# Two transformer blocks: small projections from unpadded weights, an earlier forget gate, and edits at the start, the norms, the second attention and the end

## The chip, the cores and the metric

The kernel runs on one core of a Trainium2 chip. Its time is the device time of one launch in microseconds; the median of three runs was 2513.2 (2512.42 to 2513.47).

## The reference

Two blocks in sequence on x of 256 tokens by 2048 channels, in fp32.

```python
# first block
h = rmsnorm(x, g_mix)
cb, cc, cv, q, k, v, f_logit, gate_c, gate_a = split(h @ w_in)     # f_logit: 8 columns
conv_branch = (cb * causal_dwconv(cc * cv, conv_w)) @ w_conv_out
log_f = log_sigmoid(f_logit + b_f)
attn = softmax(q k^T * scale + cumsum(log_f)_q - cumsum(log_f)_k, causal) @ v
x = x + (sigmoid(gate_c + b) * conv_branch + sigmoid(gate_a + b) * (attn @ w_attn_out)) @ w_mix_out
x = x + square(relu(rmsnorm(x, g_mlp) @ w_ff1)) @ w_ff2
x = rmsnorm(x, g_final)
# second block
mod = silu(c) @ w_ada + b_ada          # shift, scale and gate, twice
h = rms_norm(x, g) * (1 + scale_m) + shift_m
q, k, v, xs, z, B, C, dt_raw = split(h @ w_in_2)                   # dt_raw: 16 columns
attn = rms_norm(causal attention(q, k, v) with relative bias)
ssm = ssd_mixer(xs, z, B, C, dt = softplus(dt_raw + dt_bias), ...)  # state space, one chunk
x = x + gate_m * (concat(attn, ssm) @ w_out_2)
h = rms_norm(x, g) * (1 + scale_f) + shift_f
g, val = split(causal_dwconv(h @ w_up)); x = x + gate_f * ((silu(g) * val) @ w_down)
return rms_norm(x, final_norm_g)
```

## The kernel before, in words

Every product is made in split fp32: a weight piece and an activation are each written as a high part in fp32r and the remainder, and three of the four cross products are summed. A *piece* is 1 MB of weights, 128 by 2048. `piece` (L102) loads it into one of three `wraw` buffers on SP's queue, ScalarE writes the high part `wH` (L122) and VectorE the remainder `wL` (L123). With `parts=4` this goes in quarters. The loads on SP keep program order; all else is put in order, engine by engine, by a planner that works with a timeline of its own, in which `high_priority` and `behind` (an order between two instructions with no wait) are hints and bounds.

Three forms of block use pieces. `bblock` keeps weights stationary: for each half of 512 output channels, `nk` pieces, each with 16 products of 512 columns (`wH` by high part and remainder of the activation, side by side) and 16 of 256 columns (`wL` by the high part); the half is then evicted (`evict`, L177 and L179), and `acc` has two such accumulators. `ablock` keeps activations stationary, 24 products of 512 columns a piece. `wide` works on several halves at once, so that a block can begin while its activations still arrive; with `lo_first` it starts with `wL` products, which need the high parts of the activations alone. All products of these forms have line L129.

`ada` loads one row block of `w_ada` into a `wraw` buffer and multiplies it on VectorE (L99); `piece` calls it from the 19th piece on, by a count of pieces:

```python
n_pc[0] += 1
if n_ada[0] < 96 and n_pc[0] > 18 and n_ada[0] < (n_pc[0] - 18) * 0.47:
    ada()
```

`small_proj` (L255) makes the forget gate's 8 columns (`wf`) and the step size's 16 (`wdt`) from weights that the host pads to 128 columns, one piece, and transposes the result. In the first block the order is: conv inputs (`cc`, `cv`, `cb`), four pairs of a gate `gc` (four pieces) and `co` (two pieces), `wf` and the forget gate's chain on tiny tiles, q, k, v and heads, the gates `ga` and `ao`, `mix`, the feed-forward `ff1` and `ff2`. `h1_tiles` makes the first activations from x, transposed by the host, while its weights arrive; the squares for the first norm (L452, L455) are of high priority.

`norm2` makes h3 and h4, the modulated norms of the second block: for each quarter i of the channels and each half t of the tokens, x is scaled by the token's factor (`xc`, L336), transposed on TensorE (`trh`, L344), and given its affine by ScalarE (high part, L350) and VectorE (`nt`, L352, and the remainder, L354). `hold` puts the first quarter of one split behind an instruction of the norm. Between the norms stand the SSM's preparation, q, k, v with the SSM's decay and output (`yp`) in between, heads, z, and the output projection. `heads` makes for each of four heads the scores, softmax (`probs`), transposes and output (`weigh`).

At the end `down_last` multiplies the last pieces for t = 0 and 1 and each 512 channels n, adds the result to x (L970, L971), squares it (L325), and when a half of the tokens is complete scales it and writes it out (L984 to L987).

Of the kernel before, what the change touches and what calls it, by code (L numbers as in the profile page):

```python
# [13 lines left out]
P = 128  # L14
S = 256
# [9 lines left out]
_o = 0  # L25
for _n, _w in (("g_mix", 16), ("b_gate", 32), ("conv_w", 24), ("g_mlp", 16), ("b_ada", 96),
               ("norm_mix_g", 16), ("attn_norm_g", 8), ("conv_ssm_w", 48), ("conv_ssm_b", 12),
               ("d_skip", 8), ("ssm_norm_g", 8), ("norm_ffn_g", 16), ("conv_ffn_w", 264),
               ("conv_ffn_b", 88), ("dt_bias", 16), ("b_f", 8), ("a_log", 16)):
    VEC[_n] = _o  # L30
    _o += _w
# [4 lines left out]
def body(ctx: ExitStack, tc: tile.TileContext, x_d, xT_d, vec_d, con_d, rel_d, relc_d, gfin_d, c_d, fg_d,  # L36
# [149 lines left out]
    def wide(W, halves, acts, name, dst, post=None, feed=None, lo_first=False,  # L186
# [13 lines left out]
        for kg in range(2):  # L200
# [54 lines left out]
    def small_proj(w_d, n, acts, name):  # L255
        h, l = piece(w_d)
        h = h.rearrange("p a (b n) -> p (a b) n", n=P)
        l = l.rearrange("p a (b n) -> p (a b) n", n=P)
        ps = bank(name + "c")
        for f in range(2):  # L260
            for k in range(KT):
                if f == 0:
                    mm(ps[:, 0:S], h[:, k, :], acts[k][0], k == 0, False)
                    mm(ps[:, 0:S], h[:, k, :], acts[k][1], False, False)
                else:
                    mm(ps[:, 0:S], l[:, k, :], acts[k][0], False, k == KT - 1)
        c = tp.tile([P, S], F32, tag="t1k", bufs=6, name=name + "s")
        A.activation(c[0:n, :], ps[0:n, 0:S], AF.Copy)
        tr = bank(name + "t")
        for t in range(2):  # L270
            T.transpose(tr[:, t * n:(t + 1) * n], c[0:n, t * P:(t + 1) * P], ident[0:n, 0:n])
        return tr
# [56 lines left out]
    def norm2(src, r, av, bv, name):  # L329
        acts = []  # L330
        for i in range(4):
            h, l, hl = act_chunk(name, i)
            xs = []
            for t in range(2):
                xc = tp.tile([P, 512], F32, tag="t2k", bufs=4, name="xc")
                V.tensor_scalar(xc, src[i][:, t, :], r[:, t:t + 1], None,  # L336
                                op0=OP.mult)
                xs.append(xc)
            for b in range(2):
# [6 lines left out]
                for k in range(2):  # L346
                    kk = 2 * b + k
                    kt = 4 * i + kk
                    tt = tp.tile([P, S], F32, tag="t1k", bufs=6, name="nt")
                    A.activation(h[:, kk, :], ps[:, k * S:(k + 1) * S], AF.Identity,  # L350
                                 bias=bv[:, kt:kt + 1], scale=av[:, kt:kt + 1])
                    V.tensor_scalar(tt, ps[:, k * S:(k + 1) * S], av[:, kt:kt + 1],  # L352
                                    bv[:, kt:kt + 1], op0=OP.mult, op1=OP.add)
                    lt = V.tensor_tensor(l[:, kk, :], tt, h[:, kk, :].bitcast(F32), op=OP.subtract)  # L354
                    if kt == 7:
# [72 lines left out]

    h1 = []
    sq0 = []  # L430

    def h1_tiles(h, l, hl, k0, k1):
        load(xT[:, k0:k1, :], xT_d[:, k0:k1, :])
        for kt in range(k0, k1):
            k = kt % 4
            A.activation(h[:, k, :], xT[:, kt, :], AF.Copy, scale=vc("g_mix", kt))
            V.scalar_tensor_tensor(l[:, k, :], xT[:, kt, :], vc("g_mix", kt),
                                   h[:, k, :].bitcast(F32), op0=OP.mult, op1=OP.subtract)
            h1.append((h[:, k, :], l[:, k, :], hl[:, k]))
# [5 lines left out]
         feed=lambda q: h1_tiles(*chunks[q // 2], 2 * q, 2 * q + 2))  # L445
    load(vec[:, 16:], vec_d[:, 16:])
    load(con, con_d)
    with tc.high_priority():
        sacc = junk().rearrange("p (a s) -> p a s", a=2)
        for i in range(8):  # L450
            if i == 0:
                A.activation(sacc, xT[:, 0:2, :], AF.Square)  # L452
            else:
                sq = tp.tile([P, 2, S], F32, tag="t2k", bufs=4, name="sq0")
                A.activation(sq, xT[:, 2 * i:2 * i + 2, :], AF.Square)  # L455
                V.tensor_tensor(sacc, sacc, sq, op=OP.add)
# [48 lines left out]

    merged = sb.tile([P, KT, S], F32, tag="xs", name="merged")
    for j in range(4):
        g = gate(10 + j, 4 * j, f"gc{j}")

        def co_done(hf, o):  # L510
            V.tensor_tensor(merged[:, 4 * j + 2 * hf:4 * j + 2 * hf + 2, :], o,
                            g[:, 2 * hf:2 * hf + 2, :], op=OP.mult)

        bblock(wco_d, j, cy, f"co{j}", q4([P, 4, S], f"cos{j}"), co_done)


# [15 lines left out]
    cum = cp.tile([P, 16], F32, name="cum")  # L532
    A.activation(cum, cps[:, 0:16], AF.Copy)

    atc = a16("atc")
# [178 lines left out]
    def conv4(nb, ch0, name, first=False):  # L714
        raw = q4([P, 4, S], name + "r")
        if first:
            wide(win2_d, (2 * nb, 2 * nb + 1), h3, name + "p", lambda i: (raw, i), lo_first=True,
                 hold=held["h3"])
        else:
# [137 lines left out]


    for j in range(2):
        qk = []  # L860
        for hq, (nb, nm, sc) in enumerate(((0 + j, f"q2{j}", SCALE), (2 + j, f"k2{j}", None))):
# [10 lines left out]
        heads(j, qT, kT, vt, toep, lambda h, o: V.tensor_copy(cat[:, h, :], o))  # L872
    ratt = rms_ch(0, 8, 1.0 / 1024, "ratt")
# [46 lines left out]
    fg = r8("fg")  # L920
    ss4 = cp.tile([P, 2, 4], F32, name="ss4")

    def up(j):
        raw = q4([P, 4, S], f"up{j}r")
        if j == 0:
            wide(wup_d, (0, 1), h4, "up0", lambda i: (raw, i), lo_first=True, hold=held["h4"])
        else:
# [27 lines left out]
    def down_last(c, u):  # L955
        ws = [piece(wdn_d[n, c], 4, extra=None if n < 3 else True) for n in range(4)]
        rs4 = cp.tile([P, 2], F32, name="rs4")
        for t in range(2):
            ts = slice(t * P, (t + 1) * P)
            for n in range(4):  # L960
                h, l = ws[n]
                cs = slice(n * 512, (n + 1) * 512)
                ps = bank(f"dnl{t}{n}")
                for k in range(4):
                    mm(ps, u[k][0][:, ts], h[:, k, :], k == 0, False)
                    mm(ps, u[k][1][:, ts], h[:, k, :], False, False)
                for k in range(4):
                    mm(ps, u[k][0][:, ts], l[:, k, :], False, k == 3)
                tm = tp.tile([P, 512], F32, tag="t2k", bufs=4, name="tm")
                V.tensor_tensor(tm, ps, gf2[:, cs], op=OP.mult)  # L970
                V.tensor_tensor(x3[:, t, cs], x3[:, t, cs], tm, op=OP.add)  # L971
                ss_chunk(x3[:, t, cs], ss4, t, n)
                if n < 3:
                    V.tensor_tensor(x3[:, t, cs], x3[:, t, cs], fg[:, cs], op=OP.mult)
            r = rs4[:, t:t + 1]
            V.tensor_reduce(r, ss4[:, t, :], axis=AX.X, op=OP.add)
            pow_rstd(r, r, 1.0 / D)
            for n in range(4):
                cs = slice(n * 512, (n + 1) * 512)
                if n == 3:  # L980
                    V.scalar_tensor_tensor(x3[:, t, cs], x3[:, t, cs], r, fg[:, cs],
                                           op0=OP.mult, op1=OP.mult)
                elif n == 1:
                    V.tensor_scalar(x3[:, t, cs], x3[:, t, cs], r, None, op0=OP.mult)  # L984
                else:
                    A.activation(x3[:, t, cs], x3[:, t, cs], AF.Copy, scale=r)
                nc.sync.dma_start(out[0, ts, cs], x3[:, t, cs])  # L987

# [116 lines left out]
```

## Time and profile before

| | before |
|---|---|
| median of 3 runs | 2513.2 us |
| profiled execution | 2515.24 us |
| its span, first to last instruction | 2513.5 us |
| TensorE busy | 2481.0 us (99%) |
| VectorE busy | 1824.1 us (73%) |
| ScalarE busy | 1188.8 us (47%) |
| HBM read | 567.27 MB |

PE is TensorE's products, PEld its weight loads, DVE is VectorE, ACT ScalarE, POOL GpSimd, SP the queue that issues loads. Times of rows are microseconds from the start of the span. A busy share of TensorE includes products that wait in its pipeline, so the idle stretches are read from the waits and the timeline.

### The profile page before, as it was taken

Reading aid. Unit: us, or ns where it says so; the run is one execution under the profiler, and the core shown is the slowest. Engines: PE = TensorE matmul, PEld = TensorE weight load, DVE = VectorE, ACT = ScalarE, POOL = GpSimd, SP = SyncE. Lnnn points to the kernel's source line nnn. Section 1 sums busy time; section 2 is a strip of 40 time slices with the busy share of each in tenths; the row PEclk is TensorE's granted clock in tenths of the full one; section 3 lists DMA queues with packets and bytes.
Section 4 is the critical chain, followed back from the end, with each engine's and each line's share of the span. In section 5 each row is a group of like instructions: output and inputs, shape, how many; then the busy total and the mean of one; then the engine's idle time right before and its main releaser. Section 6 shows DMA issues by size and latency. Waiting matters only on the chain.

```text
span 2513.5 us, 31941 instructions
## 1 busy us (share of the span) xinstructions
PE 2481.0 (99%) x13202; PEld 2137.0 (85%) x13202; DVE 1824.1 (73%) x2011; ACT 1188.8 (47%) x1265; POOL 8.0 (0%) x16
## 2 busy tenths in 40 slices
PE   8999999999999999999998999999999999999998
PEld 7888888888888888888887888888888888888887
DVE  6787777787777777777756776575777777777768
ACT  6444444544544444444445544464544444444444
POOL 0000000000000000000000000000000000000000
PEclk9999999999999999999999999999999999999999
DMA  7677776678777777777656444455455555555553
GB/s 283 251 272 282 269 265 254 239 281 315 277 282 278 282 286 271 283 285 280 255 191 210 168 168 161 158 187 198 151 196 192 199 199 187 185 187 195 187 201 118
DMA packets 84977, 573.55 MB, mean 228 GB/s; under 512 B 9368, under 2 KB 10464, under 8 KB 16864
## 3 DMA queue, kind: packets, MB, share of 16 engines
q1 hardware_dynamic: 80352, 564.16, 61.4%
q10 hardware_dynamic: 4480, 7.36, 0.9%
q8 instruction: 103, 1.69, 0.3%
q14 instruction: 42, 0.34, 0.0%
HBM read 567.27 MB, written 4.21 MB: 227 GB/s over the span
## 4 chain that ended last, share of the span: by engine, by line
PE 96%; DVE 2%; ACT 1%; DMA 1%; issue 0%; POOL 0%; SPq 0%; ACTq 0%; POOLq 0%
PE ff L129 27%; PE up L129 20%; PE dn L129 9%; PE ga L129 4%; PE gc L129 4%; PE q L129 4%; PE k L129 4%; PE v L129 3%; PE wo L129 3%; PE mix L129 3%; PE cc L129 3%; PE z L129 2%; PE cb L129 2%; PE co L129 1%; PE ao L129 1%; PE xsc0p L129 1%
## 5 line engine op out<-in xcount | busy, mean ns | idle before, releaser
L123 DVE TENSOR_TENSOR wL<-wraw,wH 128x2048 fp32r<-128x2048 f32 (+1 forms) x511 | 998.5, 1963 | 532.8 <-ACT wH L122 524.1
L122 ACT ACTIVATE wH<-wraw 128x2048 fp32r<-128x2048 f32 (+1 forms) x511 | 837.8, 1653 | 1075.0 <-PE ff L129 359.6
L129 PE MATMUL up<-h4A,wH 128*128 128x512 f32 x1408 | 344.0, 391 | 0.0
L129 PEld LDWEIGHTS up<-h4A,wH 128*128 128x128 f32 x1408 | 256.6, 188 | 48.6 <-DVE up0r L179 0.2
L129 PE MATMUL ff<-g_mlpA,wH 128*128 128x512 f32 x1024 | 250.4, 392 | 0.0
L99 DVE SCALAR_TENSOR_TENSOR wada<-wada,c_bc 128x2048 f32<-128x2048 f32 x96 | 219.6, 2287 | 27.6 <-DMA wada<-in_wada 26.7
L129 PEld LDWEIGHTS ff<-g_mlpA,wH 128*128 128x128 f32 x1024 | 186.6, 188 | 35.7 <-issue 0.6
L129 PEld LDWEIGHTS up<-h4A,wL 128*128 128x128 f32 x1408 | 187.4, 192 | 10.3 <-ACT h4A L350 0.2
L129 PE MATMUL ff<-wH,uh 128*128 128x512 f32 x496 | 193.1, 390 | 0.0
L129 PE MATMUL ff<-wH,ul 128*128 128x512 f32 x496 | 192.9, 389 | 0.0
L129 PE MATMUL up<-h4A,wL 128*128 128x256 f32 x1408 | 191.3, 284 | 0.0
L129 PE MATMUL dn<-wH,vhl 128*128 128x512 f32 x640 | 158.3, 389 | 0.0
L129 PEld LDWEIGHTS ff<-g_mlpA,wL 128*128 128x128 f32 x1024 | 135.4, 191 | 7.4
L129 PEld LDWEIGHTS dn<-wH,vhl 128*128 128x128 f32 x640 | 119.5, 188 | 24.4
L129 PE MATMUL ff<-g_mlpA,wL 128*128 128x256 f32 x1024 | 137.9, 283 | 0.0
L129 PE MATMUL ff<-wL,uh 128*128 128x512 f32 x496 | 127.7, 389 | 0.0
L129 PEld LDWEIGHTS ff<-wH,uh 128*128 128x128 f32 x496 | 93.2, 188 | 19.4 <-issue 0.2
L129 PEld LDWEIGHTS ff<-wH,ul 128*128 128x128 f32 x496 | 93.1, 188 | 19.4 <-issue 0.2
L129 PEld LDWEIGHTS ff<-wL,uh 128*128 128x128 f32 x496 | 93.1, 188 | 19.4
L129 PE MATMUL dn<-wL,vhl 128*128 128x512 f32 x320 | 85.5, 389 | 0.0
L129 PEld LDWEIGHTS dn<-wL,vhl 128*128 128x128 f32 x320 | 60.1, 188 | 12.5
L129 PE MATMUL ga<-h1A,wH 128*128 128x512 f32 x256 | 64.6, 396 | 1.3 <-DVE aos L179 1.3
(559 smaller groups left out, 3172.2 us busy)
## 6 DMA issues: line engine op xcount, KB each, us to landing
wraw<-in_wff SPq DMA_DIRECT2D x128, 1024.0 KB, 4.8
wraw<-in_win SPq DMA_DIRECT2D x106, 1024.0 KB, 4.8
wada<-in_wada SPq DMA_DIRECT2D x96, 1024.0 KB, 4.8
wraw<-in_wup SPq DMA_DIRECT2D x88, 1024.0 KB, 4.8
wraw<-in_wdn SPq DMA_DIRECT2D x44, 1024.0 KB, 4.8
wraw<-in_wv SPq DMA_DIRECT2D x16, 1024.0 KB, 4.8
wraw<-in_wmix SPq DMA_DIRECT2D x16, 1024.0 KB, 4.9
wraw<-in_wout SPq DMA_DIRECT2D x16, 1024.0 KB, 4.8
```

Of the source, the lines that this page charges most:

```text
L99: V.scalar_tensor_tensor(w, w, 1.0, c_bc, op0=OP.mult, op1=OP.mult, accum_out=mod[:, i:i + 1])
L122: A.activation(h[:, sl], raw[:, sl], AF.Copy)
L123: ins = V.tensor_tensor(l[:, sl], raw[:, sl], h[:, sl].bitcast(F32), op=OP.subtract)
L129: return T.matmul(o, l, r, start=first, stop=last, skip_group_check=True)
```

## The change

- g_mix, 16 columns, comes with x in one array; the first two loads of x are issued by ScalarE, and the separate load is gone. All squares of x are ordered behind the last h1 tile.
- `small_proj` takes unpadded weights through small buffers, not through `piece`; high part and remainder stand side by side as one stationary operand of 2n columns; four plain products for each half of the tokens add and transpose.
- The forget gate, from `wf` to `cum`, is written ahead of the `gc` and `co` loop.
- `norm2`: ScalarE scales the first half of the tokens in quarters 1 to 3 and makes every second `nt`. `hold` has two targets: the first quarter of the second weight piece goes behind the first `xc` pair, the third piece's as before.
- In the second attention all q and k blocks, with the SSM between, come first, then v and heads for both groups.
- In `down_last` the last 512 channels of the second half of the tokens go in two halves, the norm's gain is multiplied ahead of the token factor everywhere, and outputs leave in 1024 channels.

```diff
@@ vec, xT
-    xT = sb.tile([P, KT, S], F32, tag="xs", name="xT")
+    xTg = sb.tile([P, 16 + KT * S], F32, tag="xs", name="xT")
+    xT = xTg[:, 16:].rearrange("p (k s) -> p k s", k=KT)
-    A.dma_start(vec[:, 0:16], vec_d[:, 0:16])
@@ wide
-                ws = [piece(W[hf, kg], 4, nt=8) for hf in halves]
+                ws = [piece(W[hf, kg], 4, nt=8, hold=hold[0] if hold and i else None)
+                      for i, hf in enumerate(halves)]
...
-                             hold=hold if kg == 1 and i == 0 else None)
+                             hold=hold[1] if hold and kg == 1 and i == 0 else None)
@@ small_proj
-        h, l = piece(w_d)
...
-        for f in range(2):
-            for k in range(KT):
-                if f == 0:
-                    mm(ps[:, 0:S], h[:, k, :], acts[k][0], k == 0, False)
-                    mm(ps[:, 0:S], h[:, k, :], acts[k][1], False, False)
-                else:
-                    mm(ps[:, 0:S], l[:, k, :], acts[k][0], False, k == KT - 1)
-        c = tp.tile([P, S], F32, tag="t1k", bufs=6, name=name + "s")
-        A.activation(c[0:n, :], ps[0:n, 0:S], AF.Copy)
+        raw = tp.tile([P, KT, n], F32, tag="t1k", bufs=6, name=name + "r")
+        load(raw, w_d)
+        hl = tp.tile([P, KT, 2, n], FR, tag="t2k", bufs=4, name=name + "hl")
+        split(hl[:, :, 0, :], hl[:, :, 1, :], raw)
+        for k in range(KT):
+            mm(ps[0:2 * n, :], hl[:, k].rearrange("p a n -> p (a n)"), acts[k][2], k == 0, k == KT - 1)
+        c = tp.tile([P, 2, S], F32, tag="t2k", bufs=4, name=name + "s")
+        A.activation(c[0:2 * n].rearrange("p a s -> p (a s)"), ps[0:2 * n, :], AF.Copy)
...
-            T.transpose(tr[:, t * n:(t + 1) * n], c[0:n, t * P:(t + 1) * P], ident[0:n, 0:n])
+            mm(o, c[0:2 * n, 1, ts], ident[0:2 * n, n:2 * n], t == 0, False)
+            mm(o, c[0:2 * n, 1, ts], ident[0:2 * n, 0:n], False, False)
+            mm(o, c[0:2 * n, 0, ts], ident[0:2 * n, n:2 * n], False, False)
+            mm(o, c[0:2 * n, 0, ts], ident[0:2 * n, 0:n], False, True)
@@ norm2
-                V.tensor_scalar(xc, src[i][:, t, :], r[:, t:t + 1], None, op0=OP.mult)
+                if t == 0 and i > 0:
+                    A.activation(xc, src[i][:, t, :], AF.Copy, scale=r[:, t:t + 1])
+                else:
+                    held[name] = V.tensor_scalar(xc, src[i][:, t, :], r[:, t:t + 1], None, op0=OP.mult)
+                    if i == 0:
+                        held[name + "0"] = held[name]
...
-                    V.tensor_scalar(tt, ps[...], av[...], bv[...], op0=OP.mult, op1=OP.add)
+                    if k:
+                        A.activation(tt, ps[...], AF.Identity, bias=bv[...], scale=av[...])
+                    else:
+                        V.tensor_scalar(tt, ps[...], av[...], bv[...], op0=OP.mult, op1=OP.add)
...
+            if i == 1:
+                held[name + "7"] = held[name]
@@ h1_tiles
-        load(xT[:, k0:k1, :], xT_d[:, k0:k1, :])
+        if k0 < 4:
+            A.dma_start(xTg[:, c0:c1], xT_d[:, c0:c1])
+        else:
+            load(xTg[:, c0:c1], xT_d[:, c0:c1])
@@ squares of x
-                A.activation(sacc, xT[:, 0:2, :], AF.Square)
+                behind(A.activation(sacc, xT[:, 0:2, :], AF.Square), h1_last[0])
@@ forget gate: small_proj(wf_d) down to cum, now ahead of the loop over gc and co
-    merged = ...
-    for j in range(4): ...
     fps = small_proj(wf_d, 8, h1, "wf")
...
     A.activation(cum, cps[:, 0:16], AF.Copy)
+    merged = ...
+    for j in range(4): ...
@@ second attention
+    qk = []
     for j in range(2):
-        qk = []
         for hq, (nb, nm, sc) in enumerate(...):
...
             ssm_out(j, hq, ms, last_mm[0])
-        qT, kT = qk
+    for j in range(2):
         ps = ablock(wv2_d, j, range(4), h3, f"v2{j}")
...
-        heads(j, qT, kT, vt, toep, ...)
+        heads(j, qk[2 * j], qk[2 * j + 1], vt, toep, ...)
@@ down_last
+        ss4 = cp.tile([P, 2, 5], F32, name="ss4")
+        V.memset(ss4, 0.0)
...
+                cuts = ((0, 512),) if t == 0 or n < 3 else ((0, 256), (256, 512))
+                for j, (a, b) in enumerate(cuts):
...
-                if n < 3:
-                    V.tensor_tensor(x3[:, t, cs], x3[:, t, cs], fg[:, cs], op=OP.mult)
+                    if t and n == 3:
+                        y3 = tp.tile([P, 512], F32, tag="t2k", bufs=4, name="y3") if j == 0 else y3
+                        V.tensor_tensor(y3[:, a:b], x3[:, t, cs], fg[:, cs], op=OP.mult)
+                    else:
+                        V.tensor_tensor(x3[:, t, cs], x3[:, t, cs], fg[:, cs], op=OP.mult)
...
-                nc.sync.dma_start(out[0, ts, cs], x3[:, t, cs])
+                if n % 2:
+                    cs = slice((n - 1) * 512, (n + 1) * 512)
+                    nc.sync.dma_start(out[0, ts, cs], x3[:, t, cs])
```

## Rows read from the trace of the kernel before

**Rows 1.** The page, part 1 (busy us, share) and part 4 (chain)
```profile
PE 2481.0 (99%) x13202; PEld 2137.0 (85%) x13202; DVE 1824.1 (73%) x2011; ACT 1188.8 (47%) x1265; POOL 8.0 (0%) x16
...
PE 96%; DVE 2%; ACT 1%; DMA 1%; issue 0%; POOL 0%; SPq 0%; ACTq 0%; POOLq 0%
```

**Rows 2.** TensorE's waits: engine, line, releaser, us in total, times, longest
```profile
PE cc L129 <- ACT wH L122: 6.2, 1, 6.2
PE trh L344 <- DVE xc L336: 5.4, 3, 3.1
PE trh L344 <- DVE re L706: 4.3, 1, 4.3
...
PE yp L129 <- DVE m L806: 2.0, 1, 2.0
...
PE ga L129 <- DVE aos L179: 1.3, 2, 0.7
```

**Rows 3.** The chain in order of time: start, us, what, instructions
```profile
66.76 0.79 PE rs0p L129 x8
...
281.83 4.56 PE wfc L129 x38
...
1491.10 1.47 PE yp L129 x20
...
1841.02 21.79 PE dn L129 x96
```

**Rows 4.** Timeline at the third ga gate: start, us, engine, line, instruction
```profile
523.29 2.28 DVE L99 SCALAR_TENSOR_TENSOR wada<-wada,c_bc 128x2048 f32<-128x2048 f32 x1
...
524.47 1.11 PE L129 MATMUL ao<-atc,wL 128*128 128x256 f32 x8
...
525.50 0.69 DVE L179 TENSOR_TENSOR aos<-ao,lo 128x512 f32<-128x512 f32 x1
...
526.25 0.98 PE L129 MATMUL ga<-h1A,wH 128*128 128x512 f32 x3 [0.66 <-DVE aos L179]
```

**Rows 5.** Timeline of the start
```profile
4.11 0.63 ACT L452 ACTIVATE junk<-xT 128x512 f32<-128x512 f32 x1 [1.43 <-DMA xT<-in_xT]
...
6.20 2.08 PE L129 MATMUL cc<-h1A,wH 128*128 128x512 f32 x4 [6.20 <-ACT wH L122]
7.11 0.91 ACT L436 ACTIVATE h1A<-xT,vec 128x256 fp32r<-128x256 f32 x2 [0.96 <-DMA xT<-in_xT]
```

**Rows 6.** Timeline of the norm ahead of the FFN (h4)
```profile
1764.60 1.89 DVE L123 TENSOR_TENSOR wL<-wraw,wH 128x512 fp32r<-128x512 f32 x3
...
1767.95 2.82 PE L344 MATMUL trh<-con,xc 128*128 128x128 f32 x12 [3.15 <-DVE xc L336]
```

**Rows 7.** Windows, two us within that norm: PEclk is the granted clock
```profile
1768.00:1770.00 2.00, 2.00 (x10) 2.00 (x11) 1.98 (x6) 1.02 (x2) 0.00 (x0) 0.50 0.00 0
```

**Rows 8.** Timeline of the norm ahead of the second attention (h3)
```profile
1376.17 1.28 DVE L123 TENSOR_TENSOR wL<-wraw,wH 128x512 fp32r<-128x512 f32 x2
...
1378.05 0.48 DVE L336 TENSOR_SCALAR xc<-x,rb 128x512 f32<-128x512 f32 x1
...
1390.63 27.88 SPq L62 DMA_DIRECT2D wraw<-in_win  x6
```

**Rows 9.** Timeline where yp waits
```profile
1576.73 2.29 DVE L123 TENSOR_TENSOR wL<-wraw,wH 128x2048 fp32r<-128x2048 f32 x1
```

**Rows 10.** Timeline of the tail
```profile
2504.42 0.68 DVE L970 TENSOR_TENSOR tm<-dnl,gf 128x512 f32<-128x512 f32 x1
...
2505.92 0.63 ACT L325 ACTIVATE junk<-x 128x512 f32<-128x512 f32 x1 [0.60 <-DVE x L971]
...
2508.62 1.37 SPq L987 DMA_DIRECT2D out_dram<-x  x3
```

**Rows 11.** Timeline of two passes 256 wide, near 46 us
```profile
45.65 0.38 ACT L177 ACTIVATE lo<-cc 128x256 f32<-128x256 f32 x1 [1.35 <-PE cc L129]
...
46.66 0.41 DVE L179 TENSOR_TENSOR cvs<-cc,lo 128x256 f32<-128x256 f32 x1
```

More of the change, by code (lines that the diff above doesn't have):

```diff
@@ L25 @@
 _o = 0
-for _n, _w in (("g_mix", 16), ("b_gate", 32), ("conv_w", 24), ("g_mlp", 16), ("b_ada", 96),
+for _n, _w in (("b_gate", 32), ("conv_w", 24), ("g_mlp", 16), ("b_ada", 96),
                ("norm_mix_g", 16), ("attn_norm_g", 8), ("conv_ssm_w", 48), ("conv_ssm_b", 12),
@@ L445, in body @@
          feed=lambda q: h1_tiles(*chunks[q // 2], 2 * q, 2 * q + 2))
-    load(vec[:, 16:], vec_d[:, 16:])
+    load(vec, vec_d)
     load(con, con_d)
@@ L504, in gate @@
         return bblock(win_d, nb, h1, name, q4([P, 4, S], name + "s"), done)
[L506 to L514, printed above, removed]
     fps = small_proj(wf_d, 8, h1, "wf")
@@ L533, in body, with co_done @@
     A.activation(cum, cps[:, 0:16], AF.Copy)
+    merged = sb.tile([P, KT, S], F32, tag="xs", name="merged")
+    for j in range(4):
+        g = gate(10 + j, 4 * j, f"gc{j}")
+        def co_done(hf, o):
+            V.tensor_tensor(merged[:, 4 * j + 2 * hf:4 * j + 2 * hf + 2, :], o,
+                            g[:, 2 * hf:2 * hf + 2, :], op=OP.mult)
+        bblock(wco_d, j, cy, f"co{j}", q4([P, 4, S], f"cos{j}"), co_done)
     atc = a16("atc")
@@ L717, in conv4 @@
             wide(win2_d, (2 * nb, 2 * nb + 1), h3, name + "p", lambda i: (raw, i), lo_first=True,
-                 hold=held["h3"])
+                 hold=(held["h30"], held["h37"]))
         else:
@@ L871, in body @@
             A.activation(vt[:, t, :], ps[t], AF.Copy)
-        heads(j, qT, kT, vt, toep, lambda h, o: V.tensor_copy(cat[:, h, :], o))
+        heads(j, qk[2 * j], qk[2 * j + 1], vt, toep, lambda h, o: V.tensor_copy(cat[:, h, :], o))
     ratt = rms_ch(0, 8, 1.0 / 1024, "ratt")
@@ L920, in body @@
     fg = r8("fg")
-    ss4 = cp.tile([P, 2, 4], F32, name="ss4")
     def up(j):
@@ L925, in up @@
         if j == 0:
-            wide(wup_d, (0, 1), h4, "up0", lambda i: (raw, i), lo_first=True, hold=held["h4"])
+            wide(wup_d, (0, 1), h4, "up0", lambda i: (raw, i), lo_first=True, hold=(held["h40"], held["h47"]))
         else:
@@ L961, in down_last @@
                 h, l = ws[n]
-                cs = slice(n * 512, (n + 1) * 512)
                 ps = bank(f"dnl{t}{n}")
[L964 to L972, printed above, removed]
-                if n < 3:
-                    V.tensor_tensor(x3[:, t, cs], x3[:, t, cs], fg[:, cs], op=OP.mult)
+                cuts = ((0, 512),) if t == 0 or n < 3 else ((0, 256), (256, 512))
+                for j, (a, b) in enumerate(cuts):
+                    for k in range(4):
+                        mm(ps[:, a:b], u[k][0][:, ts], h[:, k, a:b], k == 0 and j == 0, False)
+                        mm(ps[:, a:b], u[k][1][:, ts], h[:, k, a:b], False, False)
+                    for k in range(4):
+                        mm(ps[:, a:b], u[k][0][:, ts], l[:, k, a:b], False, k == 3)
+                    cs = slice(n * 512 + a, n * 512 + b)
+                    tm = tp.tile([P, 512], F32, tag="t2k", bufs=4, name="tm")
+                    V.tensor_tensor(tm[:, a:b], ps[:, a:b], gf2[:, cs], op=OP.mult)
+                    V.tensor_tensor(x3[:, t, cs], x3[:, t, cs], tm[:, a:b], op=OP.add)
+                    A.activation(junk()[:, a:b], x3[:, t, cs], AF.Square, accum_out=ss4[:, t, n + j:n + j + 1])
+                    if t and n == 3:
[3 more added lines that the diff above has]
+                        V.tensor_tensor(x3[:, t, cs], x3[:, t, cs], fg[:, cs], op=OP.mult)
             r = rs4[:, t:t + 1]
@@ L1020, in packs @@
         k, n = w.shape
-        o = np.zeros((P, KT, P), w.dtype)
-        o[:, :, :n] = w.reshape(KT, P, n).transpose(1, 0, 2)
-        return o.reshape(P, KT * P)
+        return np.ascontiguousarray(w.reshape(KT, P, n).transpose(1, 0, 2))
     def cols(a):
@@ L1031 @@
     vec = {
-        "g_mix": cols(i["g_mix"]), "b_gate": cols(i["b_gate"]), "conv_w": cols(i["conv_w"]),
+        "b_gate": cols(i["b_gate"]), "conv_w": cols(i["conv_w"]),
         "g_mlp": cols(i["g_mlp"]), "b_ada": cols(i["b_ada_2"]),
@@ L1067 @@
         "x": np.ascontiguousarray(i["x"][0]),
-        "xT": np.ascontiguousarray(i["x"][0].T.reshape(KT, P, S).transpose(1, 0, 2)),
+        "xT": np.ascontiguousarray(np.concatenate(
+            [cols(i["g_mix"]), i["x"][0].T.reshape(KT, P, S).transpose(1, 0, 2).reshape(P, KT * S)], axis=1)),
         "vec": np.ascontiguousarray(np.concatenate([vec[k] for k in VEC], axis=1)),
```

34 lines of the change are left out of this document (18 added, 16 removed).

## The prediction

> **What bounds the kernel now.** I read the page first: TensorE is busy for 2481.0 of 2513.5 us and holds 96% of the chain that ended last [rows 1]. No other engine can be late for long, so a change is worth what it takes from TensorE's own work, or from the few stretches where TensorE stands still. Next the list of TensorE's waits [rows 2]: before its first product 6.2 us, at the two norms of the second block 5.4 and 4.3, before `yp` 2.0, before a gate 0.7 twice in the row shown (and twice more behind `co`). The rest of the idle time is the tail behind the last product. Then the chain in order of time, for the price of a product in a full queue [rows 3], and the timeline at each wait. The terms below are made against the profiled execution, 2515.24 us (its span of 2513.5 and 1.8 around it). That lies 2.0 above the median of the runs, 2513.2; I subtract the sum from the median, since all terms are differences inside the span.
>
> **Small projections.** 48 products of 256 columns go, for `wf` and again for `wdt`. 38 of them took 4.56 us, 0.120 each, so 48 take 5.76; two transposes go as well, about 0.2 at the 0.099 below. In come 16 products of 512 columns at 0.227 (96 in 21.79), 3.63 us, and eight plain fp32 products that fold and transpose. An fp32 product is two passes here, and `rs0p`, four products, took 0.79 for 8 passes, 0.099 each; 16 passes are 1.58 [rows 3]. So 5.97 becomes 5.21: 0.75 less each, 1.5 for both. Bounds: at `yp`'s 1.47 for 20 passes the fold costs 1.18 and the pair saves 2.3; if TensorE waited for the copy in between (0.63 at most, a 512-column pass of ScalarE [rows 5]) the pair would save 0.2. I take 1.5, since other products are at hand at both places. The weight pieces are now 64 and 128 KB instead of two of 1 MB, which takes two long splits from ScalarE and VectorE; no gain is counted, as neither is the bound there.
>
> **Forget gate early.** TensorE's products for it are those above, moved from behind `co3` to before `gc0`; the small VectorE chain and an additional change of ScalarE's table lie beside two-group blocks and cost nothing while TensorE has a block in its queue. But `wf` was a piece, and pieces are what `ada` is counted by. Working out the condition in `piece` by hand, pieces behind `wf` get their `ada` one piece later. Before, it fell on the fourth piece of `gc2`, `gc3`, `ga2` and `ga3`, and these are the four gates whose predecessor held TensorE up; `gc1`, with `ada` on its first and third, did not. The trace shows the mechanism at `ga3`: a 2.28 us `wada` product enters VectorE just ahead of the eviction of `ao`, that starts at 525.50 instead, and TensorE's next product starts at 526.25 where eight steps of 0.12 from 524.47 would give 525.43: 0.82 lost [rows 4]. After the change `ga2` has it on its second and `ga3` on its first and third piece: both stalls should go, 1.6. `gc2` and `gc3` keep theirs. `wf` also stood between `co3` and `q0` and covered a `wada` there; `q0` has none on its fourth piece any more, so I count no new stall (0.8 if that is wrong). Bounds 0.8 worse to 1.6 better; I take 1.6.
>
> **Start.** ScalarE squares the first tile (0.63, from 4.11) ahead of the first h1 tiles; the added order puts that square behind them, and everything up to TensorE's start at 6.20 moves up, by about 0.5 (0.63 less the overlap with its successor). Two x loads leave SP's queue for ScalarE's, and the second h1 pair, which idled 0.96 for its x at 7.11, should come some 0.4 earlier [rows 5]. Together 0.9. Bounds: 0.5 worse, if the first x tile shares its transfer time with a weight quarter and lands later; 1.5 better, if all 0.96 goes as well. What moves in ScalarE's queue behind the two issues is a table load that has slack until 4.11. The Trainium skill speaks against half of this (DMA: Bandwidth & Descriptors, Issuing engines are not separate DMA queues): loads from different engines run on the same 16 DMA engines, and a second issuer saves issue time only. No row here has two issuers loading at once; by that rule the start gives 0.5 and the time would be 2505.3.
>
> **Norms.** At h4 TensorE waited 3.15 us for the second token half, then did 12 transposes in 2.82, 0.235 each, at a clock of 0.50 [rows 6, 7]. With ScalarE scaling the first half of tiles 1 to 3, four of those twelve can be done inside the wait, 4 x 0.21 = 0.85; at h3 the same four. 1.7 for both. Half of the `nt` passes also move to ScalarE, which shortens VectorE's chain; but after 1767.95 TensorE issues almost back to back at the low clock, so I count nothing for that. The added hold puts one quarter split (a third of 1.89, 0.63 [rows 6]) behind the first scaled tile in each norm; it has to be there only before the second half's products, behind 16 others. If that cover fails, 1.3 is lost: this is one bound. The other is the rival below. The `wdt` load now takes a small buffer that the norm uses too, and stands in SP's queue ahead of the next weights; before, SP had nothing to issue until 1390.63 [rows 8], so a late slot is hidden up to there, and behind it costs what it is later.
>
> **Attention of the second block.** `yp` waited 2.0 at the second group because a 2.29 us split stood ahead of the mask product on a VectorE that also ran the softmax of the first heads [rows 2, 9]. The same step in the first group, without heads beside it, shows no wait. The change puts the heads behind all four q and k blocks, so I count the 2.0 as gone, with bounds of 0 and 2.0. The heads' own work is unchanged; what is late next is in the last rival.
>
> **Tail.** The last eviction goes in two halves. Behind the last product the multiply shrinks from 0.68 to 0.41, the add likewise, the square from 0.63 to 0.38 [rows 10, 11]: 0.79 less; 24 products of 256 instead of 12 of 512 cost 2.88 against 2.72, 0.16 more. Net 0.6. Two of the four last output issues go as well; three took 1.37, 0.46 each, so up to 0.9 is saved, but a transfer of twice the size can land later by as much. I count nothing and keep 0.9 either way for the range.
>
> **Sum.** 1.5 + 1.6 + 0.9 + 1.7 + 2.0 + 0.6 = 8.3 us. 2513.2 - 8.3 = 2504.9.
>
> **Rivals.**
> The chain through the norms runs free. At h3 VectorE did three quarter splits before the scaling at 1378.05 (two took 1.28), at h4 three for 1.89 ahead of the second half's reduction [rows 6, 8]. If the new holds and the emptier VectorE let the planner put them behind, h3 starts 1.9 earlier and h4 by about half of its 1.89, since ScalarE's square runs beside them, and a shorter pause may keep the clock up. The clock of 0.50 [rows 7] follows a pause. The Trainium skill (TensorE: Matmul & The Clock Gate, Part 1) has it that idling throttles and activity releases it, and the trace agrees. The eight transposes left at each norm would take 0.235 / 2 less apiece at full clock, 1.9 for both; with 1.2 of it (an estimate, since ScalarE's share of the norm then comes last) this is 4.0 more: 2500.9. Against it: the holds bind one quarter of a piece, and the three in the way were the other quarters of a held piece. 0.14.
>
> The waits come back elsewhere. Every instruction's place is planned, and a wait taken away at one place is often given back at the next. Then the projections (1.5), the tail (0.6) and half of the start remain: 2510.6. For it: the gates' stalls came from one `ada` landing badly, so another can. Against it: the places worked out above. 0.22.
>
> Slower: heads beside `v2`. After the change the first four heads run under the second v block. A v block is 96 products, 21.8 us, in which VectorE has four splits of 2.29 [rows 3, 9], 9.2 us, and now the softmax of four heads as well. TensorE's queue is in order, so each of a head's three visits (scores, transposes, output) that meets a split waits up to the 2.0 seen at `yp`. The other terms give 6.3; four such waits undo it, six or more are slower by over 0.2%; with seven of the twelve visits late the time is 2513.2 - 6.3 + 14 = 2520.9. Against it: heads under v and gate blocks in the first attention show no wait in the list. 0.06.
>
> That the change doesn't do what it says is possible for the early gate alone (the planner may leave its products where they fit), and is part of the second rival.
>
> **Chances.** Forecast 0.58 (2502 to 2508), first rival 0.14, second 0.22, third 0.06. A measurement of this kernel can tell 0.2%, 5 us, from no change, so faster by over 0.2% is the first two, 0.72; within, 0.22; slower, 0.06. The range goes from 2500 to 2511.5: it holds the bounds of the single terms, the first two rivals, and leaves out the third.
>
> **What would show it.** `wfc` with 16 products near 3.6 us before `gc0`; `ga` gone from the list of waits while `gc` stays; no `yp` wait; TensorE's first product near 5.7; eight instead of twelve transposes behind the second half's scaling; the last square 256 wide. The forecast is wrong if new names with a microsecond or more stand in the list of waits, above all `pt` or `o` between the v blocks, or if the rows of TensorE's norms are as before.

## The result, and the profile after

The changed kernel takes 2534.9 us (median of 6 runs, 2531.7 to 2540.2) where the kernel before took 2513.9 on the same chip: a ratio of 1.0083, interval 1.0069 to 1.0097. It is slower by 0.8%. The forecast was 2504.9, the range 2500 to 2511.5; the time lies outside it on the slow side, and not at the price of the third rival (2520.9) either. The profiled execution took 2534.15, its span 2532.4.

The page of the changed kernel, to be set beside [rows 1] (busy us, share, instructions; shares of the chain that ended last):
```profile
PE 2496.5 (99%) x13178; PEld 2124.6 (84%) x13178; DVE 1811.9 (72%) x1995; ACT 1200.8 (47%) x1292; POOL 13.3 (1%) x16
...
PE 97%; DVE 1%; ACT 0%; issue 0%; POOL 0%; DMA 0%; ACTq 0%; POOLq 0%; DVEq 0%
```
TensorE has 24 instructions fewer and is busy 15.5 us longer, of the 18.9 us by which the span grew. So most of the loss lies inside its products and not in its waits.

TensorE's waits in the changed kernel (columns as in [rows 2]):
```profile
PE cc L129 <- DVE h1A L455: 7.6, 1, 7.6
PE trh L351 <- DVE xc L341: 4.5, 3, 2.3
PE rss0bp L284 <- POOL rss0r L279: 4.1, 1, 4.1
PE trh L351 <- DVE ra L723: 2.6, 1, 2.6
PE wo L129 <- ACT catA L306: 1.9, 1, 1.9
PE gc L129 <- DVE cos L179: 1.5, 2, 0.8
PE rattbp L284 <- POOL rattr L279: 1.2, 1, 1.2
...
```
`ga` and `yp` are gone, as forecast; `gc` stays, as forecast. The waits of the two norms are shorter. But the first product comes 1.4 us later, not 0.5 earlier, and `rss0bp`, `wo` and `rattbp`, all ahead of the output projection, are new names with over a microsecond, which the prediction gave as a sign of being wrong.

The chain in order of time (start, us, what, instructions), the rows that answer to [rows 3]:
```profile
152.66 3.71 PE wfc L129 x16
...
160.62 1.88 PE wft L129 x16
...
1853.79 22.39 PE dn L129 x96
```
The last row is the one to read. It is the same block of 96 products as in [rows 3], no instruction in it or beside it was edited, TensorE waits for nothing in it, and it takes 22.39 us instead of 21.79. In the changed kernel all such rows of `dn` in this part of the chain read 22.39 or 22.40; before, all read 21.79. From one product's start to the next it is 233.3 ns instead of 226.9. The changed kernel has 3732 such products of 512 columns (those of `ablock` form): 3732 x 6.4 ns = 24 us.

### The profile page after: what moved, and what is told of

The parts are those of the page before. It is cut to its first block, busy times and chain, and to the rows that moved or that the text cites. A ratio compares the mean times of both kernels' runs of the same rounds, so it can differ in the third digit from the quotient of the medians.

```text
span 2532.4 us, 31895 instructions
## 1 busy us (share of the span) xinstructions
PE 2496.5 (99%) x13178; PEld 2124.6 (84%) x13178; DVE 1811.9 (72%) x1995; ACT 1200.8 (47%) x1292; POOL 13.3 (1%) x16
## 4 chain that ended last, share of the span: by engine, by line
PE 97%; DVE 1%; ACT 0%; issue 0%; POOL 0%; DMA 0%; ACTq 0%; POOLq 0%; DVEq 0%
PE ff L129 28%; PE up L129 19%; PE dn L129 9%; PE wo L129 4%; PE gc L129 4%; PE v L129 4%; PE mix L129 4%; PE k L129 4%; PE ga L129 4%; PE q L129 4%; PE cc L129 3%; PE ao L129 2%; PE cb L129 2%; PE z L129 2%; PE co L129 1%; PE xsc0p L129 1%
## 5 line engine op out<-in xcount | busy, mean ns | idle before, releaser
L129 PEld LDWEIGHTS ff<-g_mlpA,wH 128*128 128x128 f32 x1024 | 185.9, 188 | 36.1 <-issue 0.6
L129 PE MATMUL wo<-wH,catA 128*128 128x512 f32 x256 | 66.4, 408 | 1.9 <-ACT catA L306 1.9
```

The source lines that it names most:

```text
L129: return T.matmul(o, l, r, start=first, stop=last, skip_group_check=True)
```

## Why an untouched product is slower

Between the two kernels the small tiles at the front of SBUF differ: `vec` lost 16 columns (64 bytes), `ss4` got two columns more, which take 32 bytes as placed, and x's tile grew by 16 columns (64 bytes). Every large tile behind them moved. The pieces (`wraw`, `wH`, `wL`) and the activations had all started at 224 past a multiple of 256 bytes; in the changed kernel the pieces start at 192 and everything behind x, the activations among it, at 0. The theory was that the place of a product's two operands sets its pace. Rivals were that the order of instructions had changed around the products, or other DMA traffic. Padding moves tiles and nothing else, so the runs below keep each engine's instructions and their order.

**Both back to one place.**
```diff
-    xTg = sb.tile([P, 16 + KT * S], F32, tag="xs", name="xT")
+    xTg = sb.tile([P, 64 + KT * S], F32, tag="xs", name="xT")
...
-    vec = cp.tile([P, NVEC], F32, name="vec")
+    vec = cp.tile([P, NVEC + 8], F32, name="vec")
...
```


> The changed kernel with its instructions and their order as they are; only unused columns are added (32 bytes a partition behind vec, 192 behind x), so that all large tiles again begin 96 bytes past a multiple of 128, as in the kernel before, instead of 64 (weights) and 0 (activations). Theory A (the places of the tiles in SBUF cost the time): a block of 96 products with moving weights falls from 22.39 to 21.8 us, 3,700 such products give back about 22 us, and the time falls from 2534.9 to about 2512. Theory B (the new order of the work costs the time): nothing changes, 2533 to 2537.

Ratio to before 1.0018 (1.0009 to 1.0027); the block of 96 takes 21.79. 16 of the 21 us are gone with two numbers of padding; 22 were expected, which left out the 256-column products (below).

**The kernel before, moved to the changed kernel's places** (`vec` 56 columns longer, x's tile 16).

> The kernel before with its instructions and their order as they are; unused columns put its weights 64 bytes past a multiple of 128 and its activations at a multiple, as in the changed kernel. Theory A: 96 products with moving weights rise from 21.79 to about 22.4 us and the time from 2513.9 to about 2536. Theory B: no change, 2512 to 2518.

Ratio 1.0053 (1.0038 to 1.0068), block 22.39. So the places give before's code the same block times as the changed kernel's, and the order of instructions has no part in them. The time rose by 13 us where 22 were expected, for the same reason.

**Pieces at their old place, activations at the new one** (the changed kernel, `vec` 8 longer, x's tile 56 longer).

> The changed kernel with weights 96 bytes past a multiple of 128 as before the change, and activations at a multiple as after it. If the place of the moving operand counts, the 96 products take 21.8 us and the time is near 2512, like the first run; if the place of the stationary operand counts, 22.4 us and 2535. Theory B: 2533 to 2537.

Ratio 1.0134 (1.0119 to 1.0149): slower than either. A good or a bad place of one operand alone doesn't explain that: each of the two places here stood in a run that was faster. The next two runs of the kernel before tell a distance from a place.

> The kernel before, instruction for instruction; vec is 8 columns (32 bytes) longer, so that every large tile, weights and activations alike, starts at 0 instead of 96 bytes past a multiple of 128. Theory A, the distance between the two operands counts: both still stand at the same place within 128 bytes, so a product of 512 columns in a two-group block keeps 227 ns and the time stays at before's, within 2 us. Theory B, the place itself counts (32 or 96 is good, 0 or 64 is bad): 233 ns in the two-group blocks and also in the one-group blocks, so 22 us or more, about 2538 us or above. If the places had nothing to do with it, no change, as in A, but then the next run must show none either.

> The kernel before, instruction for instruction; the tile of x is 16 columns (64 bytes) longer, so that the activations start at 32 past a multiple of 128 while the weights stay at 96. Theory A (the two operands must stand at the same place): 233 ns in the two-group blocks, 22 us more or beyond, some 2531 to 2552 us, the range of the two runs with shifted activations so far. Theory B (both stand at an odd multiple of 32, which is what counts): 227 ns and before's time within 2 us.

The first: 0.9995 (0.9986 to 1.0004). The second: 1.0058 (1.0044 to 1.0071). The same block in the chain of each, first all at 0, then activations at 32:
```profile
1844.14 21.79 PE dn L129 x96
```
```profile
1853.33 22.39 PE dn L130 x96
```
Theory A holds: the distance counts. Two more runs asked at what distance the two stand as if together again, and whether 64 past a multiple of 128 is a bad place for the pieces.

> The kernel before, instruction for instruction; the tile of x is 32 columns (128 bytes) longer, so that the activations stand 128 bytes further than the weights, counted within 256 bytes. Theory: only the place within 128 bytes counts, so 227 ns in the two-group blocks, 120 ns for the 256-column products of the one-group blocks, and before's time within 2 us. Rival: the place within 256 bytes counts, then 233 ns and some 13 to 17 us more, as with 64 bytes.

> The changed kernel, instruction for instruction; the tile of x is 48 columns (192 bytes) longer and nothing else, so that the activations stand where the changed kernel has put the weights, at 64 past a multiple of 128. Theory (the two operands' distance alone counts): 227 ns in the two-group blocks and the time of the run with both at 96, ratio to before 1.001 to 1.003, 13 to 16 us less than the changed kernel. Rival (64 is a bad place for the weights, whatever the activations do): ratio stays near 1.008.

128 bytes apart: ratio 1.0127 (1.0112 to 1.0143), my expectation of no change was wrong, and so is "within 128 bytes". Both at 192 (64 past a multiple of 128): 1.0017 (1.0008 to 1.0026), as the distance says. That run is the changed kernel with one number edited.

All spacings together, from the start times in these traces: the mean from the start of a product to the start of TensorE's next, steps over 1.25 times the median left out. The distance is the moving operand's place less the stationary one's, in bytes, counted within 256 (in the first run the activations stand 256 bytes further than before, and the pace is that of 0):

| distance | 512 columns, pieces moving (`ablock`) | 512, pieces stationary (`bblock`) | 256, pieces stationary |
|---|---|---|---|
| 0 (at 224, 0 or 192) | 226.9 ns | 229.3 | 119.2 |
| 64 | not run | 229.4 | 117.0 |
| 192 | 233.3 | not run | not run |
| 32 | not run | 233.3 | 116.9 |
| 224 | 233.3 | not run | not run |
| 128 | 232.4 | 232.7 | 118.9 |

In the changed kernel the pieces stand at 192 and activations at 0, so `ablock` products (pieces move) have distance 192 and lose 6.4 ns, all but 12 of the 3732, 24 us; the 4416 products of 256 columns have distance 64 and gain 2.2 ns, 9.7 us; as many of 512 columns lose 0.1, 0.4 us. Net 14.6 us, where the run with one number edited gives back 0.0066 of 2514, 16.6. The same sum gives 14.7 for the kernel before at the changed places and again with activations at 32 (measured 13.3 and 14.6), 34.3 for 128 bytes apart (32.0), and 31.4 between the first run and the one with pieces at their old place and activations at the new (29.2). Why a distance does this no run here shows: that two reads of one memory meet would be a guess.

**Used the other way round.** The table offers a gain: distance 0 where pieces move, 64 where they are stationary.
```diff
-        hl = sb.tile([P, 4, 2, S], FR, tag="act", bufs=4, name=f"{name}A{i}")
+        off = 16 if name in ("h1", "g_mlp", "h3", "h4") else 0
+        hl = sb.tile([P, 64 + 8 * S], FR, tag="act", bufs=4, name=f"{name}A{i}")
+        hl = hl[:, off:off + 8 * S].rearrange("p (k b s) -> p k b s", k=4, b=2)
```


> The kernel before, instruction for instruction, with the same two places: activations of the one-group blocks 64 bytes past the weights, all others at the weights' place. Theory: 6.7 us (0.27%) faster than before by the same sum. Rival: 2 to 4 us slower, if only the losses come.

2510.6 us against 2517.1, ratio 0.9972 (0.9961 to 0.9983): 6.5 us gained where 6.7 were worked out, with no instruction added, dropped or moved. The groups of 256-column products before, then of this run (busy us, mean ns of one, which includes the pipeline):
```profile
L129 PE MATMUL up<-h4A,wL 128*128 128x256 f32 x1408 | 191.3, 284 | 0.0
```
```profile
L131 PE MATMUL up<-h4A,wL 128*128 128x256 f32 x1408 | 187.8, 280 | 0.0
```
This run also answers the rival that other tiles, which moved along in the runs before, set the pace, for it moves some operands and leaves others. From start to start these `up` products went from 119.3 to 116.8 ns; `co` and `ao`, whose activations kept their place, stayed at 119.0. The two v blocks of the first and the two of the second attention, whose distance became 192, went from 227.0 to 233.3, and all other products with pieces moving stayed at 226.9.

## The rest of the change

With the places out of the way, the parts can be read. The same stages in five profiled executions, cut at first products (us; a norm's stage begins at the last product ahead of it and ends at the first `wH` product behind it); "old places" is the first run above, "old attention" and "old start, tail" are the two runs below:

| stage | before | changed | old places | + old attention | + old start, tail |
|---|---|---|---|---|---|
| to the first product | 6.20 | 7.58 | 7.99 | 7.98 | 5.53 |
| to `ga` | 422.99 | 423.05 | 421.25 | 422.07 | 424.01 |
| `ga`, `ao` | 141.86 | 138.83 | 139.87 | 139.87 | 139.88 |
| `mix`, feed-forward, to the norm's inputs | 802.89 | 810.89 | 800.16 | 800.16 | 800.15 |
| norm h3 | 15.30 | 13.62 | 15.84 | 13.65 | 13.64 |
| to q | 72.37 | 71.93 | 72.23 | 72.21 | 72.23 |
| q, v, heads, z | 212.06 | 213.26 | 213.36 | 212.01 | 213.63 |
| `wo` | 88.84 | 97.29 | 94.55 | 88.85 | 88.84 |
| norm h4 | 14.49 | 13.56 | 15.79 | 15.75 | 14.03 |
| `up`, `down` | 705.33 | 709.24 | 705.25 | 705.25 | 704.51 |
| last block and tail | 31.14 | 33.10 | 32.60 | 32.59 | 31.12 |
| span | 2513.5 | 2532.4 | 2518.9 | 2510.4 | 2507.6 |

**Second attention back in the old order** (heads of the first group ahead of the second group's q).
```diff
-    qk = []
     for j in range(2):
+        qk = []
...
-    for j in range(2):
         ps = ablock(wv2_d, j, range(4), h3, f"v2{j}")
...
-        heads(j, qk[2 * j], qk[2 * j + 1], vt, toep, ...)
+        heads(j, qk[0], qk[1], vt, toep, ...)
```


> As the first run, and the second attention in its old order (heads of a group behind its own q, k and v). Theory A with the late heads as the second cause: the stall ahead of the output projection (about 9 us between the last z block and the projection's steady products) goes, the wait of yp (2 us) returns, and the time is 6 to 8 us under the first run, near 2505, my forecast. Theory B: the attention alone is the cause, and this run is 20 us under the first.

Ratio 0.9996 (0.9986 to 1.0006) where the run with the new order has 1.0018: the new order costs some 5 us (6 to 8 were expected). The table puts it at `wo`, 5.7 (the stage ahead of it varies by 1.6 between the two executions in the old order). TensorE's waits agree: at the old places the new order has `rss0bp` 4.4, `wo` 1.9 and `rattbp` 1.2 and is without `yp`'s 2.0, together 5.5. The timeline there in the changed kernel:
```profile
1679.17 0.79 PE L129 MATMUL wo<-wH,catA 128*128 128x512 f32 x1 [1.89 <-ACT catA L306]
1679.44 0.15 DVE L277 TENSOR_SCALAR rss0r<-rss0p 128x2 f32<-128x2 f32 x1
1679.52 1.21 DVE L901 TENSOR_TENSOR cat<-cat,zs 128x1024 f32<-128x1024 f32 x1
1679.67 4.34 POOL L279 TENSOR_TENSOR rss0r<-rss0r,mhalf 128x2 f32<-128x2 f32 x1 [6.90 <-DVE rss0r L277]
1680.65 2.48 DVE L307 TENSOR_TENSOR catA<-cat,catA 128x512 fp32r<-128x512 f32 x4
...
1683.06 0.41 DVE L854 TENSOR_TENSOR rss1a<-rss1a,sq 128x256 f32<-128x256 f32 x1
...
1684.07 0.69 PE L284 MATMUL rss0bp<-con,rss0r 128*128 128x128 f32 x2 [4.11 <-POOL rss0r L279]
```
The last head's output is copied at 1669.5, 51 us behind z's first product; before it was 38 us behind. So the two norms of the concatenated heads and SSM, which `wo` needs, come when VectorE has all of `wo`'s inputs to make. And GpSimd's power of 128 by 2, which the kernel before did in 0.69 at this place, takes 4.34, with `rss0bp` waiting for it and the rest of `wo`'s first products behind that (the next starts at 1684.41). It starts 0.15 behind the first of six VectorE instructions in a row and ends at 1684.01, 0.54 behind the last of them. In the kernel before it started 0.15 ahead of the VectorE instruction beside it:
```profile
1678.44 0.69 POOL L277 TENSOR_TENSOR rss0r<-rss0r,mhalf 128x2 f32<-128x2 f32 x1 [13.22 <-DVE rss0r L275]
...
1678.59 1.23 DVE L883 TENSOR_TENSOR cat<-cat,zs 128x1024 f32<-128x1024 f32 x1 [0.23 <-ACT zs L881]
```
The theory was that VectorE, working back to back on pairs of SBUF tiles, keeps GpSimd from reading.
```diff
...
         pow_rstd(r, ps[:, 0:2], inv_n)
+        if name == "rss0":
+            held["rss0"] = V.tensor_copy(r4[:, 2:4], r)
...
-        V.tensor_tensor(cat[:, sl, :], cat[:, sl, :], z, op=OP.mult)
+        ins = V.tensor_tensor(cat[:, sl, :], cat[:, sl, :], z, op=OP.mult)
+        if j:
+            behind(ins, held["rss0"])
...
-        V.tensor_tensor(l, src, h.bitcast(F32), op=OP.subtract)
+        ins = V.tensor_tensor(l, src, h.bitcast(F32), op=OP.subtract)
+        if prev is not None:
+            behind(ins, prev)
...
```


> The changed kernel at the old places (new attention order kept); between the two engines one thing is new: VectorE copies the first SSM norm's token factor (128 x 2) as soon as GpSimd has written it, and the multiply by z and the four remainders of the output projection's activations stand behind that copy, in the same order as before. Theory: GpSimd's small power took 4.34 us because VectorE worked back to back on products of two SBUF tiles and kept GpSimd from reading; with VectorE standing still it takes 0.5 to 1.0 us, TensorE's wait for it falls from 4.4 to below 1.5, and the run is 2 to 3 us shorter than the same kernel without the copy, about 2518.5. Rival: the power is slow at this place for another reason (the engine had been idle for long, the clock of the engine): it takes 4.3 us again, VectorE waits as long, and the run is 2 to 4 us longer, 2523 to 2525.

Ratio 0.9999 (0.9991 to 1.0008) against 1.0018. Its timeline:
```profile
1674.31 0.69 POOL L279 TENSOR_TENSOR rss0r<-rss0r,mhalf 128x2 f32<-128x2 f32 x1 [6.87 <-DVE rss0r L277]
...
1675.05 0.43 PE L284 MATMUL rss0bp<-con,rss0r 128*128 128x128 f32 x2 [0.75 <-POOL rss0r L279]
...
1676.98 1.22 PE L129 MATMUL wo<-wH,catA 128*128 128x512 f32 x2 [1.50 <-DVE catA L307]
```
The power takes 0.69 once VectorE stands still, with GpSimd idle as long before it as in the slow case (6.87 and 6.90), so the rival of the long idle time is out: shown. The Trainium skill (SBUF — State Buffer, Who interferes with whom) states that a VectorE instruction with two SBUF inputs and a GpSimd instruction that reads SBUF shut each other out; the trace agrees, with 4.34 against 0.69. Of TensorE's wait 4.4 become 0.75, but 1.50 comes back on the remainders that VectorE now makes later: 2.2 gained by the waits, 1.2 by the `wo` stage in the profile, and 4.8 by the ratios, with some 3 either way. So how much of the new order's cost is GpSimd's step stays open between 1 and 5 us; that the rest is the late heads was read from the trace and not tried by itself.

**Start and last block back as before** (`g_mix` by itself, x on SP's queue, squares free, last 512 channels whole, outputs in 512 channels).

> The changed kernel at the old places, with the second attention, the start (g_mix by itself, x on the load queue, squares not ordered) and the last block as they were before: left of the change are the small projections, the early forget gate and the norms. Theory: the new start costs 1.8 us (first product at 7.98 instead of 6.20) and the halved last eviction with merged outputs about 1.4 (the lead at the last block's first product, 4.5 us, was 3.0 at the end). So 3 us less than the run with new start and tail: some 3 us (0.1%) faster than before, first product near 6.2, end near 2508 in the profile. Rival: the start is a delay that the first block absorbs and the tail only moves its end, then this is the same as that run, 0 to 1 us from before.

2512.5 us against 2517.0, ratio 0.9983 (0.9974 to 0.9991): faster than both kernels, as expected. The first product is at 5.53, the last stage 31.12. What is left of the change here, small projections, early gate and norms, is worth 4.5 us (0.17%), with what else they moved (`tps`, next).

**With the two places as well.**

> The run with old start, tail and attention order; here the activations of the one-group blocks (h1, g_mlp, h3, h4) stand 64 bytes past the weights, and all others, which the two-group blocks load as stationary operands, at the weights' place. From the spacings so far: about 4160 products of 256 columns gain 2.5 ns each (10.4 us), as many of 512 columns lose 0.3 (1.2 us), and the 384 of the two v blocks, which use h1 and h3, lose 6.4 (2.5 us): 6.7 us less than that run. So about 11 us (0.44%) faster than before. Rival: the 256-column gain belongs to shifted scratch tiles and not to the pair of operands, then 120 ns stay and the run is some 2 us slower than the one it is made from, 0.1% faster than before.

2509.3 us, ratio 0.9965 (0.9952 to 0.9977), the fastest version; 7.8 us gained where 11 were expected. Its profile shows `tps`, products late in the feed-forward, waiting 2.9 us for a DMA, and the stretch from there to the last feed-forward block takes 40.9 us, where the run without the two places took 36.1. Whether that is the missing 3 us is open. All six profiles of the kernel before and of its forms with other places have this wait (2.1 to 3.5 us); of the eight profiles of the changed kernel and its forms two have it (this one, and 2.4 in the run with the power ahead). So the change takes it away in most executions, a gain of 2 to 3 us that no term of the forecast names; its cause was not looked for.

## Why the prediction was wrong

- **The step that failed** is the first: a change "is worth what it takes from TensorE's own work, or from the few stretches where TensorE stands still". The sum priced the instructions removed, added and moved, and took some 12,600 untouched products at their old pace. The change moved their operands in SBUF; 16 of the 21 us are that, shown by the runs that move tiles alone: 233.3 ns instead of 226.9 for a product with pieces moving. Edits worked out at nothing (a vector 64 bytes shorter) were the dearest.
- **Small projections, -1.5.** 16 products took 3.71 (forecast 3.63) and the fold 1.88 (1.58), 0.38 less than the 5.97 that went, so 0.8 for both. By the stage that holds `wdt` (to q) it is 0.15 at the old places, 0.3 for both; `wf`'s stage (to `ga`) varies by 2.8 between executions and can't tell. Either is within the bounds.
- **Forget gate, -1.6.** Right: both `ga` waits are gone, `gc` keeps its two, the stage is 2.0 shorter at the old places.
- **Start, -0.9.** Wrong in sign: +1.4 in the changed kernel, +1.8 at the old places. The first product came at 7.6 to 8.0 in the six profiles with the new start, at 5.5 to 6.7 in the eight with the old. The first x tile, issued by ScalarE at the moment when SP issues two weight quarters, landed 5.6 us after its issue; before, alone in front, 3.3. First the landing times of x before, then of the changed kernel, then the changed kernel's start:
```profile
DMA to landing us min/median/max: 3.3/5.4/6.3
```
```profile
DMA to landing us min/median/max: 5.6/6.6/6.8
```
```profile
0.73 0.43 ACTq L449 DMA_DIRECT2D xT<-in_xT  x1
...
5.77 0.63 ACT L122 ACTIVATE wH<-wraw 128x512 fp32r<-128x512 f32 x1 [3.07 <-DMA wraw<-in_win]
6.40 0.91 ACT L454 ACTIVATE h1A<-xT 128x256 fp32r<-128x256 f32 x2
```
  The bound of 0.5 worse named this very case and was too small: the first x tile lands 2.3 later by its own issue, and the h1 tiles now come behind `wH`. The Trainium skill's rule cited there (DMA: Bandwidth & Descriptors, Issuing engines are not separate DMA queues), that a second issuer saves issue time only, agrees with these rows.
- **Norms, -1.7.** The size is near in the changed kernel (-1.7 at h3, -0.9 at h4) and not at the old places (+0.5 and +1.3, where the clock stayed low for longer: 0.50 over 10 us at h3). The mechanism is that of the first rival, and the term's own (four transposes moved into the wait; at the 0.235 beside it, 0.94 each and not 0.85) didn't come. At h4 twelve transposes still stand behind the second scaling; the three quarter splits of [rows 6] went behind it, and the pause shrank from 3.15 to 2.28:
```profile
1781.03 2.59 PE L351 MATMUL trh<-con,xc 128*128 128x128 f32 x12 [2.28 <-DVE xc L341]
1781.28 2.49 DVE L123 TENSOR_TENSOR wL<-wraw,wH 128x512 fp32r<-128x512 f32 x4
```
  How long the clock then stays low differs between executions. The same norm in the changed kernel and at the old places, the window in which the granted clock comes back from 0.50, the lower of its two levels, to 1.00 (PEclk, the third number from the end):
```profile
1784.00:1786.00 2.00, 1.19 (x9) 0.90 (x8) 2.00 (x6) 1.67 (x5) 0.00 (x0) 0.82 0.99 418
```
```profile
1778.00:1780.00 2.00, 2.00 (x15) 2.00 (x15) 0.98 (x4) 1.15 (x4) 0.00 (x0) 0.76 0.00 0
```
  These windows lie 3 to 5 us behind the first of the twelve transposes in the one (1781.03) and 8 to 10 in the other (1769.85); the norm takes 13.56 and 15.79 us.
- **Second attention, -2.0.** The `yp` wait went, as forecast, and more came back: from q to the end of `wo` 300.90 us before, 300.86 and 302.47 in the two runs in the old order, 307.91 in the new order at the old places. "What is late next" was looked for at `v2`, where no wait appeared. It was one step further: the norms of the heads, and GpSimd.
- **Tail, -0.6.** Measured +1.5. The two halves are written into one tile, and the second half's products wait 0.5 for the first half's multiply; behind them VectorE does a 0.68 multiply by the gain, which the change had moved there, ahead of the last add:
```profile
2520.91 1.69 PE L129 MATMUL dnl<-wHL,vhl 128*128 128x256 f32 x12 [0.52 <-DVE tm L991]
...
2523.56 0.41 DVE L991 TENSOR_TENSOR tm<-dnl,gf 128x256 f32<-128x256 f32 x1
...
2523.90 0.68 DVE L998 TENSOR_TENSOR x<-x,fg 128x512 f32<-128x512 f32 x1
...
2525.01 0.42 ACT L993 ACTIVATE junk<-x 128x256 f32<-128x256 f32 x1 [0.80 <-DVE x L992]
```

The terms as measured at the old places, -0.3 - 2.0 + 1.8 - 2.1 + 5.7 + 1.5, are +4.6 with the norms at their better value; the runs gave 1.0018, 4.5 us. That they meet is in part choice: with the norms as they were in the profile at the old places (+1.8) the sum is +8.5 where its span grew by 5.4, and the difference lies in other stages, 2.2 of it from `tps` on.

## What to carry to other kernels

When a change adds, drops or resizes any tile, compare where the large tiles start before and after, and look in both profiles at a long block that nobody touched: if its time moved and nothing in it waits, try padding that puts the tiles back. When work is put later on one engine to clear a wait, follow it to its next consumer, here two blocks further on, and look what else that stretch asks of the engine. A small GpSimd step that starts just behind the first of several VectorE steps on pairs of SBUF tiles can take several times its own length (4.34 us for 0.69 here).

## What was not expected of the hardware

- The pace of a product depends on the distance of its two operands in SBUF, counted within 256 bytes: 226.9 ns at 0, 232.4 at 128, 233.3 at 192 and at 224, for 512 columns with pieces moving. With pieces stationary, 64 bytes cost 0.1 ns at 512 columns and gain 2.2 at 256.
- A GpSimd operation on 128 by 2 elements took 4.34 us when it started 0.15 us behind the first of six VectorE instructions in a row, 0.69 with VectorE standing still, and 0.69 when it started 0.15 ahead of one.
- After the same pause at the same place, the granted clock came back from 0.50 3 to 5 us behind the first transposes in one execution and 8 to 10 in another.
